# A first product with three tiles of the indexer's queries instead of two, in units of two k, and a smaller tile to warm TensorE

## The chip, the cores and the metric

The kernel runs on one core of one Trainium2 chip. A core has TensorE (PE in the profile, its weight loads PEld), VectorE (DVE), ScalarE (ACT), GpSimd (POOL) and SyncE (SP, here a queue that issues transfers). The metric is the device time of one execution in microseconds: 1672.79 us is the median of three runs before the change (1672.7 to 1672.99).

## The reference

One layer of a streaming encoder over 512 frames with 2048 channels, in float32. The normalised input goes through one wide projection, whose parts feed a sparse attention, a retention mixer and gates. The part that matters here is the indexer of the sparse attention: 16 heads of 64 channels (`iq`), one key of 64 channels (`ik`) and 16 weights (`iw`).

```python
h = rmsnorm(x, norm_gain)
proj = h @ w_in
(aq, ak, av, az, iq, ik, iw, rq, rk, rv, rz, ga, gb) = jnp.split(proj, SPLIT_POINTS, axis=-1)
...
iq = iq.reshape(B, L, IDX_HEADS, IDX_DIM) * (IDX_DIM ** -0.5)
ik = plain_layernorm(ik)
...
score = jnp.einsum('bqhd,bsd->bqsh', qi_c, ki)
index = jnp.einsum('bqsh,bqh->bqs', jax.nn.relu(score), w_c).astype(jnp.float32)
...
_, sel = lax.top_k(index, topk)
```

Behind it come the gather of the chosen keys, softmax, the retention, the output projections, a gated addition and a last RMSNorm.

## The kernel before

**Precision.** A float32 operand is split in two: `h`, the value rounded to the type that TensorE takes (`fp32r`), written by ACT (L153 for weights, L413 for the input), and `l`, the rest, written by DVE (L158, L414). A product is the sum of three matmuls: h with h, h with l, l with h (L214 to L216). `wh` and `wl` are the parts of a weight, `hh` and `hl` those of the input.

**Units.** Weights are loaded in units of some k (slices of 128 input channels, 16 in all). `block` registers the units of a matrix, `load_to` issues their transfers on SP's queue, and `split_to` emits the ACT instruction at once and the DVE one a step later. The raw tiles have 7 buffers (small units among the first four take another kind), `wh` and `wl` 3 each. `gemms` runs several products over the same input side by side: for each k it goes through its jobs, three matmuls each, and calls `step()` after each job. At the first k of a unit it splits units ahead: 2 from the current one in the first product, 3 in all others.

**Order.** The instructions of each engine run in the order in which this program emits them (`manual_schedule`), and each engine waits where an operand isn't ready. `todo` is a list from which each `step()` takes one entry (often empty); `later(n, f)` runs `f` n steps on; `bg` is a background list taken from when `todo` is empty.

**The head.** ACT's queue loads the gains; SP's queue loads the slices `xk` of the input and the units of `w_ik` in turn, in an order set by a list of k (L370). `w_ik` has 80 columns for the key and the weights and 256 for the first two tiles (of 128 columns, two heads) of the indexer's queries, in units of 1, 2, 2, 2, 3, 3 and 3 k. DVE sets `ones`, `mhalf` and `warm`; ten matmuls on `warm` (L408) keep TensorE busy until the first operands are there. `x_split` (L410) splits slice k of the input. Two slices and two units are split ahead of the first product; from there, the later slices stand in `todo`, a slice every three steps, with the squares for the RMSNorm between them (`rms_acc`).

The first product has three jobs: `ps_ikw` (80 columns, 512 frames) and two `ps_iq` (128 columns, the 384 frames for which a choice has to be made), so 9 matmuls and 3 steps a k. Then `kraw` is copied by ACT and each tile goes through `iq_split`: two ACT copies and two DVE subtractions. The six other tiles of the queries follow as products of their own, of 16 steps, in units of 8 k. Between them, from `todo`, come the sum of squares (`f_sum`), the RMSNorm's factor (`f_rnat`, `f_bcast`), the key's layernorm (`f_keys1` to `f_keys3`) and the scores of each tile (`index_tile`); by `later`, counted from the end of the first product, positions (`f_pos`), the bias table (`f_table1`, `f_table2`) and the rotary angles (`f_rope1`, `f_turns`, `f_rope2`). Then come the values (`ps_vn`), and the rest of the layer.

Of the kernel before, what the change touches and what calls it, by code (L numbers as in the profile page):

```python
# [11 lines left out]
BF = mybir.dt.bfloat16  # L12
# [5 lines left out]
L = 512  # L18
D = 2048
KT = D // 128  # L20
# [15 lines left out]
def block_kernel(tc, xT, pT, posb, posq, w_in, w_v, w_ik, w_a, w_b, w_o, w_ple, w_gate,  # L36
                 w_gt, w_pt, fgb, tab, gains, cst, dec, out, out_a, out_b):
    nc = tc.nc
    pe, dve, act, pool, sp = nc.tensor, nc.vector, nc.scalar, nc.gpsimd, nc.sync

    with contextlib.ExitStack() as ctx:
# [10 lines left out]
        def U(name, dt=F32):  # L52
            return up.tile([128, L], dt, name=name, tag="u")
# [26 lines left out]
        def block(src, chunks, cols=128):  # L80
            ids, k0 = [], 0
            for nk in chunks:
                ids.append(len(units))
                units.append((raw(src, k0, nk, cols), None, nk, cols))
                k0 += nk
            return ids
# [84 lines left out]
        todo = collections.deque()  # L171
# [27 lines left out]
        def gemms(jobs, ahead=None, order=None, each=None):  # L199

            pss = [P(j[4]) for j in jobs]
            seqs = [ksteps(j[0]) for j in jobs]
            late = order is not None
            order = order or range(len(seqs[0]))
            for s in order:
                for ps, seq, (_, w, parts, c, _) in zip(pss, seqs, jobs):
                    i, k = seq[s]
                    if k == 0:
                        split_to(i + (ahead or AHEAD) - (late and s > 0))
                        load_to(i + AHEAD + LOADS)  # L210
                    h, l = loaded[i]
                    a, b = parts[s][0][:, c], parts[s][1][:, c]
                    o = ps[:w.stop - w.start, c]
                    pe.matmul(o, h[:, k, w], a, start=(s == order[0]), stop=False)  # L214
                    pe.matmul(o, h[:, k, w], b, start=False, stop=False)  # L215
                    pe.matmul(o, l[:, k, w], a, start=False, stop=(s == order[-1]))  # L216
                    step()
                if each is not None:
                    each(s)
            return pss  # L220

        ALL = slice(0, L)
# [115 lines left out]
        K8 = (8, 8)  # L338
        col = lambda g, m: w_in[g + m]
        AQ, AK, AZ, IQ, RQ, RK, RZ, GA, GB = 0, 8, 16, 24, 32, 40, 48, 56, 72  # L340
        u_ik = block(w_ik, (1, 2, 2, 2, 3, 3, 3), 336)
        u_iq = [None, None] + [block(col(IQ, m), K8) for m in range(2, 8)]
        u_rv = [block(w_v[i], (2,) * 8, 512) for i in range(2)]
        u_av = block_wide_pair(w_v[2], w_v[3])
        u_r, u_g = [], []
        for h in range(NH):
            u_r.append(block_pair(col(RQ, h), col(RK, h)))
            for n in (2 * h, 2 * h + 1):
                g, m = ((GB, 2 * n), (GA, 2 * n - 16))[n >= 8]
# [17 lines left out]
        ng, fg, gn = g_sb[:, 0:16], g_sb[:, 16:32], g_sb[:, 32:40]  # L367
        xs = []
        for k in range(KT):
            if k in (1, 2, 3, 5, 7, 9, 12):  # L370
                load_to(state["raw"] + 1)
            if k < 10:
                t = U("xk")
                sp.dma_start(t, xT[:, k, :])
                xs.append(t)
            elif k % 2 == 0:
                t = B("xk2")
                sp.dma_start(t[:, 0:1024].rearrange("p (a c) -> p a c", a=2), xT[:, k:k + 2, :])
                xs += [t[:, 0:512], t[:, 512:1024]]
# [2 lines left out]
        pos_i = U("pos_i", I32)  # L382
        posq_i = cp.tile([128, 128], I32, name="posq_i")
        tb = cp.tile([128, 66], F32, name="tb")
        ones = cp.tile([128, 128], F32, name="ones")
        dve.memset(ones, 1.0)
        mhalf = cp.tile([128, 16], F32, name="mhalf")
# [5 lines left out]
        def rms_acc(src, k, c=ALL):  # L393
            sq = U("sq")
            act.activation(sq[:, c], src, AF.Square)
            i = k % 2
            if acc[i] is None:
                acc[i] = sq
            else:
                (pool, dve)[i].tensor_add(acc[i][:, c], acc[i][:, c], sq[:, c])  # L400

        warm = U("warm", BF)
        dve.memset(warm, 0.0)
        wact = cp.tile([128, 16], F32, name="wact")
        act.activation(wact, mhalf, AF.Copy)
        ps_w = P("ps_warm")
        for i in range(WARM):
            pe.matmul(ps_w, warm[:, 0:128], warm, start=(i == 0), stop=(i == WARM - 1))  # L408

        def x_split(k):  # L410
            h = U("hh", F32R)
# [37 lines left out]
        for k in range(2, KT):  # L449
            todo.append(lambda k=k: x_split(k))  # L450
            if k > 2:
                todo.extend([None, None if k % 2 else lambda k=k: rms_acc(xs[k // 2 - 2], k // 2 - 2)])
        for k in range(6, KT):
            todo.extend([lambda k=k: rms_acc(xs[k], k), None])

        ps_ikw, *ps_iq01 = gemms([(u_ik, slice(0, 80), hparts, ALL, "ps_ikw")]
                                 + [(u_ik, slice(a, a + 128), hparts, slice(128, L), "ps_iq") for a in (80, 208)], 2)

        def iq_split(ps):
            ta = U("ta", F32R)  # L460
# [7 lines left out]
        R = {}  # L468
        kraw = U("kraw")
        act.activation(kraw[:80, :], ps_ikw[:80, :], AF.Copy)  # L470
        ix = [iq_split(ps) for ps in ps_iq01]

        def f_sum():
            dve.tensor_add(acc[0], acc[0], acc[1])
# [119 lines left out]
            R["ct"], R["st"] = ct, st  # L594

        N3 = [None] * 3
        todo.extend(N3 * 3 + [f_sum] + N3 * 3 + [f_rnat] + N3 * 3 + [f_bcast, None, f_keys1] + N3 * 3 + [f_keys2] + N3 * 2 + [f_keys3] + N3 * 2)
        later(80, f_pos)
        later(88, f_table1)
        later(92, f_table2)  # L600
# [47 lines left out]
            load = [lambda: xn_load(k + 1)] if k < 7 else []  # L648
            return load + [lambda: xn_norm(k)] + [lambda i=i: h_step(k, i) for i in range(X_STEPS)]

        for m in range(2):
            index_tile(m, ix[m])
        for m in range(2, 8):
            ix = iq_split(gemm(u_iq[m], hparts, "ps_iq", slice(128, L)))
            index_tile(m, ix)

# [752 lines left out]
WARM = 10  # L1409
# [8 lines left out]
def _layout(x, p, positions, w_in, norm_gain, w_a_out, w_b_out, w_o, ret_gn_gain,  # L1418
            w_ple, w_ple_gate, rel_bias, final_gain):
    import numpy as np  # L1420
    f32 = np.float32

    def tiles(w, c=128):
        k, n = w.shape
        return np.ascontiguousarray(w.reshape(k // 128, 128, n // c, c).transpose(2, 1, 0, 3))

    def chans(v):
        return v.reshape(-1, 128).T

    w = np.asarray(w_in)[0]  # L1430
    o = {}
    o["xT"] = np.ascontiguousarray(np.asarray(x)[0].T.reshape(KT, 128, L).transpose(1, 0, 2))
    o["pT"] = np.ascontiguousarray(np.asarray(p)[0, 0].T.reshape(2, 128, L).transpose(1, 0, 2))
    pos = np.asarray(positions)[0]
    o["posb"] = np.ascontiguousarray(np.broadcast_to(pos[None, :], (128, L)))
    o["posq"] = np.ascontiguousarray(np.repeat(pos.reshape(128, 4).T, 32, axis=0))
    o["w_in"] = np.concatenate([tiles(w[:, a:b]) for a, b in
                                ((0, 2048), (3072, 5120), (5200, 7248), (8272, 13392))])
    o["w_v"] = np.concatenate([tiles(w[:, a:a + 1024], 512) for a in (7248, 2048)])
    o["w_ik"] = np.ascontiguousarray(  # L1440
        np.concatenate([w[:, 5120:5200], w[:, 4096:4352]], axis=1).reshape(KT, 128, 336).transpose(1, 0, 2))
    o["w_a"] = tiles(np.asarray(w_a_out)[0])
    o["w_b"] = tiles(np.asarray(w_b_out)[0])
    o["w_o"] = tiles(np.asarray(w_o)[0])
    o["w_ple"] = np.ascontiguousarray(
        np.asarray(w_ple)[0].reshape(2, 128, 16, 128).transpose(1, 2, 0, 3).reshape(128, 32, 128))
    o["w_gate"] = tiles(np.asarray(w_ple_gate)[0])
    o["w_gt"] = tiles(np.asarray(w_ple_gate)[0][:, 1536:], 512)
    o["w_pt"] = tiles(np.asarray(w_ple)[0][:, 1536:], 512)
    o["fgb"] = np.ascontiguousarray(np.broadcast_to(np.asarray(final_gain)[None, 1536:], (128, 512)))  # L1450
    tab = np.asarray(rel_bias)
    t = np.zeros((128, 66), f32)
    for q in range(4):
        for b in range(31):
            t[32 * q + b, 8 * q:8 * q + 8] = tab[ROW[b]]
            t[32 * q + b, 32 + 8 * q:40 + 8 * q] = tab[ROW[b - 1]]
        t[32 * q:32 * q + 32, 64] = [-1e9] + [i - 0.5 for i in THR[1:]] + [1e9]
        t[32 * q:32 * q + 32, 65] = [1.0] + [-1.0] * 31
    o["tab"] = t
    o["gains"] = np.ascontiguousarray(np.concatenate(  # L1460
        [chans(np.asarray(norm_gain)[0]), chans(np.asarray(final_gain)), chans(np.asarray(ret_gn_gain)[0])], axis=1))
    c = np.zeros((128, 130), f32)
    c[:, :128] = np.eye(128)
    c[:, 128] = np.tile((10000.0 ** (-np.arange(64) / 64.0)).astype(f32), 2)
    c[:, 129] = math.pi / 2
    o["cst"] = c
    s = np.arange(128)[:, None]
    q = np.arange(128)[None, :]
    dec = np.zeros((128, NH, 257))
    for h in range(NH):  # L1470
        g = math.log(1.0 - 2.0 ** (-5.0 - h))
        dec[:, h, :128] = np.where(q // 64 >= s // 64, np.exp(g * np.abs(q - s)), 0.0) * 128.0 ** -0.5
        dec[:, h, 128:256] = np.exp(g * (q + 1.0))
        dec[:, h, 256] = np.exp(g * (127.0 - s[:, 0])) * 128.0 ** -0.5
    o["dec"] = dec.astype(f32)
    return o
# [30 lines left out]
```

## Time and profile before

| | us |
|---|---|
| median of three runs | 1672.79 |
| profiled execution, its own time | 1672.5 |
| its span, first to last instruction | 1670.7 |
| PE busy | 1659.0 |
| DVE busy | 1255.5 |
| ACT busy | 934.8 |
| POOL busy | 251.7 |

Rows of the timeline give the start, the duration, engine, source line, operation, and output and inputs with shapes; in brackets stands how long the engine was idle before and what released it. The ends of matmuls are modelled and overlap the next one, so a rate is read from the starts. A row of the waits gives the total time, the number of waits and the longest one. A row of the windows gives, for a stretch of time, the busy time and count of PE, PEld, DVE, ACT and POOL, then the granted clock, the share of the DMA engines and GB/s. A row of the transfers gives their count, the size of one and the median time from issue to landing. Of the changes below, the profile's lines before L386 keep their numbers in the kernel after; those behind move by up to two.

### The profile page before, as it was taken

To read this page: it belongs to the slowest core of one execution; us is meant where nothing else is said; L and a number is where in the kernel's file an instruction comes from. 1 tells how busy PE (TensorE), PEld (TensorE's weight loads), DVE (VectorE), ACT (ScalarE), POOL (GpSimd) and SP (SyncE) were. 2 spreads that over 40 slices of the span, in tenths; PEclk is the share of its full clock that TensorE was granted. 3 is DMA by queue.
4 is the path that set the end of the run, shared out by engine and by line. 5 is a ranking of instruction groups with operands and counts; after the bars stand their busy time and mean duration, and the time that the engine had idled before them with its cause. 6 is when DMAs were issued, how large, how long until landed. Compare 5 with 4: busy or idle time off the path is not lost.

```text
span 1670.7 us, 24613 instructions
## 1 busy us (share of the span) xinstructions
PE 1659.0 (99%) x9160; PEld 1442.3 (86%) x9160; DVE 1255.5 (75%) x1912; ACT 934.8 (56%) x1424; POOL 251.7 (15%) x267
## 2 busy tenths in 40 slices
PE   9999999999999999999999999999999999999997
PEld 7988888888888888888888888888888888888896
DVE  7798789888888888777776676777678877864453
ACT  7465545555555555777766665566634544463342
POOL 2100112111111111111331112100000111012222
PEclk9999999999999999999999999999999999999998
DMA  7328989788788788788988888997466788732223
GB/s 290 127 89 256 321 233 275 189 209 218 193 205 216 192 204 217 192 228 243 239 236 221 220 223 226 255 363 276 150 227 189 194 215 221 203 107 101 88 64 101
DMA packets 122568, 343.26 MB, mean 205 GB/s; under 512 B 13712, under 2 KB 22800, under 8 KB 122448
## 3 DMA queue, kind: packets, MB, share of 16 engines
q1 hardware_dynamic: 85792, 229.98, 39.9%
q0 software_dynamic: 25712, 92.03, 29.3%
q10 hardware_dynamic: 10944, 19.69, 3.3%
q8 instruction: 72, 1.18, 0.3%
q14 instruction: 48, 0.39, 0.1%
HBM read 300.21 MB, written 41.42 MB: 204 GB/s over the span
## 4 chain that ended last, share of the span: by engine, by line
PE 95%; DVE 2%; ACT 2%; issue 1%; DMA 0%; POOL 0%; SPq 0%; POOLq 0%; ACTq 0%; DVEq 0%
PE ps_p L284 24%; PE ps_v L284 16%; PE ps_r L284 8%; PE ps_q L284 8%; PE ps_w L215 3%; PE ps_w L214 3%; PE ps_w L216 3%; PE ps_pg L216 3%; PE ps_pg L215 3%; PE ps_pg L214 3%; PE ps_vn L757 2%; PE ps_vn L758 2%; PE ps_vn L759 2%; PE ps_iq L214 1%; PE ps_iq L216 1%; PE ps_iq L215 1%
## 5 line engine op out<-in xcount | busy, mean ns | idle before, releaser
L158 DVE TENSOR_TENSOR wl<-wraw,wh 128x1024 fp32r<-128x1024 f32 (+2 forms) x459 | 563.0, 1239 | 176.2 <-ACT wh L153 174.5
L153 ACT ACTIVATE wh<-wraw 128x1024 fp32r<-128x1024 f32 (+2 forms) x459 | 474.4, 1043 | 234.4 <-DVE wraw L160 114.0
L119 POOL DMA_DIRECT2D wraw<-w_in x120 | 106.5, 958 | 572.2 <-DVE wl L158 321.1
L284 PE MATMUL ps_p<-hs,wh 128*128 128x512 f32 x640 | 161.4, 393 | 0.0
L247 ACT ACTIVATE e<-ps_p 128x512 f32<-128x512 f32 x144 | 86.0, 597 | 113.9 <-PE ps_p L284 112.5
L284 PEld LDWEIGHTS ps_p<-hs,wh 128*128 128x128 f32 x640 | 114.8, 189 | 21.0 <-issue 0.6
L284 PE MATMUL ps_p<-hs,wl 128*128 128x256 f32 x640 | 92.0, 284 | 0.0
L284 PEld LDWEIGHTS ps_p<-hs,wl 128*128 128x128 f32 x640 | 83.1, 192 | 0.3 <-issue 0.3
L284 PE MATMUL ps_q<-ha,wh 128*128 128x512 f32 x320 | 80.4, 393 | 0.0
L284 PE MATMUL ps_v<-ha,wh 128*128 128x512 f32 x320 | 80.1, 392 | 0.0
L284 PE MATMUL ps_r<-hs,wh 128*128 128x512 f32 x320 | 79.3, 390 | 0.4 <-ACT wh L153 0.4
L284 PE MATMUL ps_p<-ha,wh 128*128 128x512 f32 x320 | 79.6, 390 | 0.0
L284 PE MATMUL ps_v<-hs,wh 128*128 128x512 f32 x320 | 79.0, 389 | 0.0
L689 ACT ACTIVATE mk<-relf,thr 128x512 f16<-128x512 f32 (+3 forms) x128 | 68.2, 555 | 14.7 <-DVE go L977 10.2
L216 PE MATMUL ps_pg<-rh,wl 128*128 128x512 f32 x192 | 74.8, 390 | 0.0
L215 PE MATMUL ps_pg<-rl,wh 128*128 128x512 f32 x192 | 74.7, 389 | 0.0
L214 PE MATMUL ps_pg<-rh,wh 128*128 128x512 f32 x192 | 74.7, 389 | 0.0
L119 POOL DMA_DIRECT2D wraw<-w_o x24 | 21.1, 942 | 348.6 <-DVE wl L158 316.4
L977 DVE TENSOR_TENSOR go<-e_t 128x256 f32<-128x256 f32 x160 | 68.0, 425 | 5.7
L251 DVE TENSOR_TENSOR e_t<-ps_p,pv 128x512 f32<-128x512 f32 x48 | 33.1, 690 | 51.5 <-ACT e L247 51.5
L284 PEld LDWEIGHTS ps_r<-hs,wh 128*128 128x128 f32 x320 | 59.8, 188 | 13.8 <-ACT wh L153 1.4
L284 PEld LDWEIGHTS ps_p<-ha,wh 128*128 128x128 f32 x320 | 59.9, 188 | 13.0 <-issue 0.6
(412 smaller groups left out, 3739.2 us busy)
## 6 DMA issues: line engine op xcount, KB each, us to landing
wraw<-w_in SPq DMA_DIRECT2D x172, 512.0 KB, 5.2
wraw<-w_in POOLq DMA_DIRECT2D x120, 512.0 KB, 8.1
wraw<-w_v SPq DMA_DIRECT2D x32, 512.0 KB, 4.1
wraw<-w_o SPq DMA_DIRECT2D x32, 512.0 KB, 4.8
wraw<-w_o POOLq DMA_DIRECT2D x24, 512.0 KB, 6.3
wraw<-w_gate SPq DMA_DIRECT2D x24, 512.0 KB, 3.9
wraw<-w_b SPq DMA_DIRECT2D x16, 512.0 KB, 6.1
wraw<-w_a SPq DMA_DIRECT2D x16, 512.0 KB, 4.1
```

The costliest lines, as they stand in the source:

```text
L119: pool.dma_start(out=view(raw_tiles[r], nk, cols), in_=src[:, k0:k0 + nk, :], accum_op=OP.add)
L153: act.activation(h, raw, AF.Copy)
L158: dve.tensor_sub(l, raw, h.bitcast(F32))
L214: pe.matmul(o, h[:, k, w], a, start=(s == order[0]), stop=False)
L215: pe.matmul(o, h[:, k, w], b, start=False, stop=False)
L216: pe.matmul(o, l[:, k, w], a, start=False, stop=(s == order[-1]))
L247: act.activation(E[n], src, AF.Copy)
L284: pe.matmul(o[:, c], w[:, k], X[PRODUCTS[n]][k][:, c], start=(n < 4 and first and k == 0), stop=(ended[n] == 16), skip_group_check=True)
L689: act.activation(bias_e[b][:, ln * i:ln * i + ln], relf[:, :ln], AF.Sign, bias=thr[:, q:q + 1])
L757: pe.matmul(pss[t], a[:, tok(t)], h[:, k], start=(s == 0), stop=False)
L758: pe.matmul(pss[t], a[:, tok(t)], l[:, k], start=False, stop=False)
L977: dve.tensor_add(o[:, q], c0, c1)
```

## The change

A third tile of the indexer's queries (tile 2) is computed in the first product, which so has four jobs, 12 matmuls and 4 steps a k. The matrix `w_ik` is 464 columns wide instead of 336 and comes in units of 1, 1 and then seven times 2 k; the order of the loads follows. Tile 2 has no product of its own any more. The list of steps gets one empty step for each of the slices 3 to 7, and three empty steps fewer ahead of `f_sum`. `warm` is 128 columns instead of 512, is set first of DVE's tiles, and the warming matmuls read its 128 columns four times over.

```diff
-        u_ik = block(w_ik, (1, 2, 2, 2, 3, 3, 3), 336)
-        u_iq = [None, None] + [block(col(IQ, m), K8) for m in range(2, 8)]
+        u_ik = block(w_ik, (1, 1) + (2,) * 7, 464)
+        u_iq = [None] * 3 + [block(col(IQ, m), K8) for m in range(3, 8)]
...
-            if k in (1, 2, 3, 5, 7, 9, 12):
+            if k in (1, 2, 3, 5, 7, 9, 11, 13, 15):
                 load_to(state["raw"] + 1)
...
+        warm = U("warm", BF)[:, 0:128]
+        dve.memset(warm, 0.0)
         ones = cp.tile([128, 128], F32, name="ones")
         dve.memset(ones, 1.0)
...
-        warm = U("warm", BF)
-        dve.memset(warm, 0.0)
...
-            pe.matmul(ps_w, warm[:, 0:128], warm, start=(i == 0), stop=(i == WARM - 1))
+            pe.matmul(ps_w.rearrange("p (a c) -> p a c", a=4), warm, warm[:, None, :].to_broadcast([128, 4, 128]),
+                      start=(i == 0), stop=(i == WARM - 1))
...
-                todo.extend([None, None if k % 2 else lambda k=k: rms_acc(xs[k // 2 - 2], k // 2 - 2)])
+                todo.extend([None, None if k % 2 else lambda k=k: rms_acc(xs[k // 2 - 2], k // 2 - 2)] + [None] * (k < 8))
...
-        ps_ikw, *ps_iq01 = gemms([(u_ik, slice(0, 80), hparts, ALL, "ps_ikw")]
-                                 + [(u_ik, slice(a, a + 128), hparts, slice(128, L), "ps_iq") for a in (80, 208)], 2)
+        ps_ikw, *ps_iqs = gemms([(u_ik, slice(0, 80), hparts, ALL, "ps_ikw")]
+                                 + [(u_ik, slice(a, a + 128), hparts, slice(128, L), "ps_iq") for a in (80, 208, 336)], 2)
...
-        ix = [iq_split(ps) for ps in ps_iq01]
+        ix = [iq_split(ps) for ps in ps_iqs]
...
-        todo.extend(N3 * 3 + [f_sum] + N3 * 3 + [f_rnat] + N3 * 3 + [f_bcast, None, f_keys1] + N3 * 3 + [f_keys2] + N3 * 2 + [f_keys3] + N3 * 2)
+        todo.extend(N3 * 2 + [f_sum] + N3 * 3 + [f_rnat] + N3 * 3 + [f_bcast, None, f_keys1] + N3 * 3 + [f_keys2] + N3 * 2 + [f_keys3] + N3 * 2)
...
-        for m in range(2):
+        for m in range(3):
             index_tile(m, ix[m])
-        for m in range(2, 8):
+        for m in range(3, 8):
             ix = iq_split(gemm(u_iq[m], hparts, "ps_iq", slice(128, L)))
             index_tile(m, ix)
...
-        np.concatenate([w[:, 5120:5200], w[:, 4096:4352]], axis=1).reshape(KT, 128, 336).transpose(1, 0, 2))
+        np.concatenate([w[:, 5120:5200], w[:, 4096:4480]], axis=1).reshape(KT, 128, 464).transpose(1, 0, 2))
```

## The prediction

> **What bounds the kernel now.** I began with the page: its busy shares and its chain of waits.
>
> ```profile
> span 1670.7 us, 24613 instructions
> PE 1659.0 (99%) x9160; PEld 1442.3 (86%) x9160; DVE 1255.5 (75%) x1912; ACT 934.8 (56%) x1424; POOL 251.7 (15%) x267
> PE 95%; DVE 2%; ACT 2%; issue 1%; DMA 0%; POOL 0%; SPq 0%; POOLq 0%; ACTq 0%; DVEq 0%
> ```
>
> TensorE is the bound. A change that keeps its matmuls can only win back the 11.7 us in which PE is not busy (1670.7 less 1659.0), or open new waits. So the second view is PE's list of waits over the whole span, its three longest rows and the one of this stage:
>
> ```profile
> PE ps_b L1378 <- POOL rl L1374: 3.5, 1, 3.5
> PE ps_warm L408 <- DVE warm L403: 1.4, 1, 1.4
> PE ps_r L284 <- ACT wh L153: 0.4, 2, 0.2
> PE ps_ikw L216 <- DVE wl L158: 0.2, 1, 0.2
> ```
>
> The largest is in the tail, which the diff leaves alone. A busy PE hides waits for weights, so the third view is the timeline of the head, read by the starts of the matmuls.
>
> ```profile
> 0.84 0.17 DVE L386 MEMSET ones<- 128x128 f32 x1 [0.84 <-PEq L1498]
> 0.95 0.07 DVE L388 MEMSET mhalf<- 128x16 f32 x1
> 1.03 0.27 DVE L403 MEMSET warm<- 128x256 uint32 x1
> ...
> 1.36 4.45 PE L408 MATMUL ps_warm<-warm 128*128 128x512 bf16 x10 [1.36 <-DVE warm L403]
> ...
> 4.49 0.47 ACT L153 ACTIVATE wh<-wraw 128x336 fp32r<-128x336 f32 x1
> ...
> 5.17 0.25 PEld L214 LDWEIGHTS ps_ikw<-hh,wh 128*80 128x80 f32 x1 [0.28 <-ACT wh L153]
> ...
> 6.03 0.63 PE L215 MATMUL ps_ikw<-hl,wh 128*80 128x512 f32 x1
> 6.46 0.50 PE L216 MATMUL ps_ikw<-hh,wl 128*80 128x512 f32 x1
> ...
> 6.79 0.34 PE L214 MATMUL ps_iq<-hh,wh 128*128 128x384 f32 x1
> ...
> 7.20 0.77 ACT L153 ACTIVATE wh<-wraw 128x672 fp32r<-128x672 f32 x1 [1.15 <-DMA wraw<-w_ik]
> 8.00 0.86 DVE L158 TENSOR_TENSOR wl<-wraw,wh 128x672 fp32r<-128x672 f32 x1 [1.17 <-ACT wh L153]
> ...
> 8.91 0.46 PE L216 MATMUL ps_ikw<-hh,wl 128*80 128x512 f32 x1 [0.20 <-DVE wl L158]
> 9.21 0.34 PE L214 MATMUL ps_iq<-hh,wh 128*128 128x384 f32 x1
> 9.57 0.73 ACT L413 ACTIVATE hh<-xk,g_sb 128x512 fp32r<-128x512 f32 x1 [0.81 <-DMA xk<-xT]
> 10.21 0.75 ACT L153 ACTIVATE wh<-wraw 128x672 fp32r<-128x672 f32 x1
> 10.26 0.39 PE L214 MATMUL ps_ikw<-hh,wh 128*80 128x512 f32 x1
> ...
> 12.00 0.39 PE L214 MATMUL ps_ikw<-hh,wh 128*80 128x512 f32 x1
> ```
>
> Four readings. A 512-column matmul costs 0.43 us at first (6.03 to 6.46, and 4.45 over ten), so the warming ends about 1.36 + 4.27 = 5.63 and the real work starts near 5.60; TensorE runs at full speed from about 6.7. One k takes 1.74 us (10.26 to 12.00): three keys matmuls, 0.69 together, and two tiles at 0.52 each. Step k=0 should end at 6.79 + 1.05 = 7.84, and k=1 should reach its tiles at 7.84 + 0.69 = 8.53. They come at 9.21: **0.68 us lost**, to the second unit, which lands only at 7.20 and whose wl ends at 8.86. After that this stage loses nothing: k=2 lives on the same unit, and the third, split by ACT from 10.21 behind k=3's hh, is wanted only at 12.00.
>
> **The change part by part.** *Tile moved.* 48 matmuls of 384 columns move from a product of their own into the first one; none is added. In both places three take 0.52 us, and the 16 slices of 128 columns to split replace two units of 1024. In matmul time: 0.
>
> *Warming.* A memset of 64 words lies between those of 16 (0.07) and 128 (0.17): 0.11. It is now first, from 0.84, so it ends at 0.95, and with the 0.06 that the row shows up to the matmul the warming starts at 1.01 and ends at 5.28, 0.35 earlier. But the first unit is now 464 columns wide. Its split, between 0.47 (336) and 0.77 (672), takes 0.58, so from 4.49 it ends at 5.07; before, 4.96 was followed by matmuls only at 5.60 because of the warming. Adding the 0.2 until PE's weight load begins and the 0.25 of the load, work starts at 5.52. **Gain 0.08 us** (bounds 0 and 0.35). That the ten matmuls read one block four times has no row; I take 0.43 each, since the number of columns is the same. Doubled, it would cost 4.3 us.
>
> *Units of (1, 1, 2, ...).* With three tiles a k takes 1.74 + 0.52 = 2.26 us. k=0 runs from 5.52: 1.19 as before until its tiles (5.60 to 6.79), then 1.57, so to 8.28. The second unit is smaller (cumulated 976 KB to its end, against 1016), so its wh is ready by 7.8 and its wl by 8.5, before the third matmul of k=1 at 8.74: **the old 0.68 goes**. k=1 ends at 10.54. Now k=2 needs the *third* unit, and ACT's order is still hh of k=2, hh of k=3, then this wh.
>
> ```profile
> 8.00:10.00 2.00, 1.78 (x9) 1.26 (x9) 1.55 (x2) 1.15 (x2) 0.00 (x0) 1.00 1.03 393
> ...
> wraw<-w_ik SPq DMA_DIRECT2D x3, 336.0 KB, 5.8
> ...
> wraw<-w_ik SPq DMA_DIRECT2D x1, 168.0 KB, 3.0
> ...
> 15.09 1.03 ACT L153 ACTIVATE wh<-wraw 128x1008 fp32r<-128x1008 f32 x1
> 16.15 1.21 DVE L158 TENSOR_TENSOR wl<-wraw,wh 128x1008 fp32r<-128x1008 f32 x1 [0.18 <-ACT wh L153]
> ```
>
> The x of k=3 landed at 9.57 after 4 x 256 + 168 + 336 + 336 = 1864 KB; now 1952 KB go ahead, and 88 KB at 393 GB/s are 0.23 us: 9.80. The wh follows 0.64 later (9.57 to 10.21), at 10.44, and for 928 columns (between 0.75 and 1.03) takes 0.97: 11.41. PE, ready at 10.54, starts k=2 at about 11.46: **0.92 us lost**. The wl then takes 1.12 (between 0.86 and 1.21), to 12.57; by the row of before the tiles follow 0.35 after a wl's end (8.86 to 9.21), at 12.92 instead of 11.46 + 0.69 = 12.15: **0.77 us lost**. Behind this ACT and DVE have 4.5 us for each unit and need about 3.3, so nothing more. Balance of the head: -0.08 - 0.68 + 0.92 + 0.77 = **+0.93 us** (bounds -0.76, if the third unit came in time, and +1.7, if both matmul waits were half as long again).
>
> *The turn into the next product.* Only one unit of it is split ahead; the second waits behind what is done with the first product's results.
>
> ```profile
> 33.84 0.59 ACT L470 ACTIVATE kraw<-ps_ikw 80x512 f32<-80x512 f32 x1 [5.33 <-PE ps_ikw L216]
> ...
> 34.68 0.35 PE L214 MATMUL ps_iq<-hh,wh 128*128 128x384 f32 x1
> ...
> 35.38 0.55 DVE L464 TENSOR_TENSOR ta<-ps_iq,ta 64x384 fp32r<-64x384 f32 x1 [2.51 <-ACT tz L463]
> ...
> 37.67 2.36 DVE L158 TENSOR_TENSOR wl<-wraw,wh 128x1024 fp32r<-128x1024 f32 x2
> ...
> 39.21 0.33 PE L216 MATMUL ps_iq<-hh,wl 128*128 128x384 f32 x1
> ```
>
> Count from the end T of the first product (34.68). DVE's first subtraction starts at T + 0.70, four take 2.29, the first of two wl ends at T + 4.17, and the matmul that reads it starts at T + 4.53: 0.36 spare, about 0.2 of it the weight load. With a third tile the keys' result is ready 0.52 earlier before T, so the first subtraction starts at T + 0.18; six take 3.43, and the wl ends at T + 4.79. Queued behind these subtractions are this wl and the next; PE waits for the first: 0.26 + 0.2 = **0.45 us lost** (bounds 0 and 1.1, two subtractions' time). The next unit has a further 4 us.
>
> *Shifts behind it.* Position, table and rotary steps are counted from the end of the first product and come 16 steps later; the index tasks behind them by 2.
>
> ```profile
> 57.44 1.05 PE L432 MATMUL ps_bc<-cs,r_nat 128*128 128x128 f32 x8
> ...
> 84.17 0.42 DVE L538 CAST relf<-rel_i 128x512 f32<-128x512 int32 x1
> ...
> 85.47 0.20 DVE L547 MAX8 d<-da 128x8 f32<-128x32 f32 x1
> ...
> 88.96 0.38 PE L554 MATMUL ps_d<-cs,d 128*128 128x128 f32 x2
> ...
> 119.79 0.41 DVE L593 TENSOR_SCALAR st<-st 64x512 f32<-64x512 f32 x1
> ...
> 100.00:110.00 10.00, 10.00 (x49) 8.43 (x48) 9.50 (x15) 4.48 (x9) 0.00 (x0) 1.00 0.35 106
> ```
>
> The matmul on the table has 3.3 us of cover and keeps its eight steps. DVE is 95% busy in the values' stage, into which these steps move, but PE does not wait there: nothing, as long as the split units ahead cover it. SP's constants now stand behind two more weight loads, some 2 us, against a first use at 57.44. Of the 0.4 us of waits at ps_r, a shifted order could remove all or add as much: 0 taken.
>
> **Sum.** +0.93 + 0.45 = +1.4 us. The profiled execution took 1672.5 us (1.8 around its span of 1670.7), 0.3 below the median of 1672.79. Against that median: **1674.2 us, 0.08% more**, within the 0.2% (3.3 us) that a measurement here tells from no change.
>
> **The rivals.** *The third unit arrives in time.* For it: DMA moves faster than the bytes ask once running, and the early units of weights come in longer rows. Against: x of k=3 waited for its DMA, and ACT works in order. If the waits at k=2 vanish, -0.76 + 0.45 = -0.3: 1672.5 us.
>
> *The clock falls back.* Waits of 0.92 and 0.77 us within 2.4 us, just after full speed was reached, could return TensorE to half speed. The first rise took from 1.36 to about 6.7, 5.3 us; as long again at half speed costs 2.65, so 1674.2 + 2.65 = 1676.9, slower than before. [...] Against it: before, 0.68 us idle at 8 us left the spacing at 0.17. The Trainium skill (TensorE: Matmul & The Clock Gate, "Why this matters for your kernels") asks for idle gaps of over about 3 us before the rate halves; by that rule neither gap is enough and the sum stays 1674.2.
>
> *The values' stage falls behind.* The steps that move there, from the row at 84.17 to the one at 119.79, are 26 instructions of DVE with 9.4 us together. If DVE's idle 5% doesn't absorb them in time and a wl comes late by a third of it, 3 us: 1677. Against it: units there are split three ahead, and the steps leave a stage where DVE was as full.
>
> **How the numbers follow.** Forecast 0.62 (own range 1673.3 to 1675.3, from the bounds at k=2 and the turn), third unit in time 0.18, clock 0.09, values' stage 0.08, anything else 0.03. Faster by over 0.2% needs more than the head ever lost: 0.02. Slower by over 0.2% (above 1676.1) takes the two slow rivals and the forecast's upper edge, 0.09 + 0.08 + 0.03 = 0.20; within is 0.78. The range 1672.2 to 1676.6 holds the forecast and the first rival, and leaves most of the slow ones out.
>
> **What would show it.** Right: warming from about 1.0 us; no gap at k=1; k=2's first matmul near 11.5, behind ACT's wh, its tiles near 12.9; the first product ending near 43.9 us; a short PE wait on wl some 4.5 us after. Wrong: k=2 back to back, spacing of 0.43 us after 12 us, or PE waits past 90 us that were not there.

## The result and the profile after

| | before | after |
|---|---|---|
| median of 21 runs each | 1672.60 us | 1675.36 us |
| lowest to highest | 1671.77 to 1673.34 | 1674.48 to 1676.10 |
| profiled execution: its own time, span | 1672.5, 1670.7 | 1675.02, 1673.3 |

The ratio is 1.0016, 95% interval 1.0010 to 1.0022: the change costs 2.8 us. The forecast had +1.4 us. The page of the kernel after says what still bounds it:

```profile
span 1673.3 us, 24614 instructions
PE 1659.8 (99%) x9160; PEld 1441.9 (86%) x9160; DVE 1252.7 (75%) x1912; ACT 933.6 (56%) x1424; POOL 250.2 (15%) x267
```

The count of matmuls is the same and PE is busy 0.8 us more; the other 1.8 of the 2.6 us of span are new idle time. PE's list of waits over the whole span of the kernel after tells where (total us, count, longest):

```profile
PE ps_b L1379 <- POOL rl L1375: 3.5, 1, 3.5
PE ps_r L284 <- ACT wh L153: 1.4, 3, 0.7
PE ps_warm L408 <- DVE warm L386: 1.0, 1, 1.0
PE ps_ikw L216 <- DVE wl L158: 0.5, 1, 0.5
PE ps_ikw L214 <- ACT wh L153: 0.3, 1, 0.3
PE ps_iq L216 <- DVE wl L158: 0.2, 1, 0.2
```

The tail's 3.5 is unchanged and the warming's wait is shorter. The rows of `ps_ikw` and `ps_iq` are the head and the turn, which the prediction had. The row it took at nothing is the second: `ps_r`, one of the paired products (L284) far behind the edit, waits 1.4 us in place of 0.4. The weight loads show the same at more places; their rows of the same view, before and then after:

```profile
PEld ps_r L284 <- ACT wh L153: 1.4, 3, 0.6
```

```profile
PEld ps_r L284 <- ACT wh L153: 3.4, 5, 1.2
```

**The head.** The timeline of the kernel after:

```profile
1.00 4.45 PE L408 MATMUL ps_warm<-warm 128*128 128x512 bf16 x10 [1.00 <-DVE warm L386]
...
6.09 0.45 PE L216 MATMUL ps_ikw<-hh,wl 128*80 128x512 f32 x1
...
6.39 0.34 PE L214 MATMUL ps_iq<-hh,wh 128*128 128x384 f32 x1
...
8.65 0.34 PE L214 MATMUL ps_iq<-hh,wh 128*128 128x384 f32 x1
...
9.02 0.72 ACT L414 ACTIVATE hh<-xk,g_sb 128x512 fp32r<-128x512 f32 x1 [1.16 <-DMA xk<-xT]
...
9.65 0.96 ACT L153 ACTIVATE wh<-wraw 128x928 fp32r<-128x928 f32 x1
...
10.06 0.34 PE L216 MATMUL ps_iq<-hh,wl 128*128 128x384 f32 x1
...
10.64 1.13 DVE L158 TENSOR_TENSOR wl<-wraw,wh 128x928 fp32r<-128x928 f32 x1
...
10.66 0.46 PE L214 MATMUL ps_ikw<-hh,wh 128*80 128x512 f32 x1 [0.27 <-ACT wh L153]
...
11.82 0.46 PE L216 MATMUL ps_ikw<-hh,wl 128*80 128x512 f32 x1 [0.48 <-DVE wl L158]
...
12.12 0.34 PE L214 MATMUL ps_iq<-hh,wh 128*128 128x384 f32 x1
```

The tiles of k=0 come at 6.39, where before had 6.79; those of k=1 at 8.65, with no gap; k=2 starts at 10.66 instead of 10.06 + 0.17 = 10.23, behind ACT's wh, and its tiles at 12.12 instead of 10.66 + 0.69 = 11.35, behind DVE's wl. So k=2 loses 0.43 + 0.77 = 1.20 us.

**The turn.** The timeline of the kernel before, at the first matmul behind its third tile (48 matmuls behind 34.68), and then that of the kernel after, at the same place of the work:

```profile
43.03 0.33 PE L214 MATMUL ps_iq<-hh,wh 128*128 128x384 f32 x1
...
1659.52 0.39 PE L1313 MATMUL ps_tw<-wh,pl 128*128 128x512 f32 x1
```

```profile
43.15 0.33 PE L214 MATMUL ps_iq<-hh,wh 128*128 128x384 f32 x1
...
46.74 2.36 DVE L158 TENSOR_TENSOR wl<-wraw,wh 128x1024 fp32r<-128x1024 f32 x2
...
47.48 0.34 PE L215 MATMUL ps_iq<-hl,wh 128*128 128x384 f32 x1
...
48.02 0.44 PE L216 MATMUL ps_iq<-hh,wl 128*128 128x384 f32 x1 [0.20 <-DVE wl L158]
...
1661.64 0.39 PE L1314 MATMUL ps_tw<-wh,pl 128*128 128x512 f32 x1
```

Read by the starts of the same matmul, the head costs 43.15 - 43.03 = 0.12 us, and the turn 48.02 - 47.66 = 0.36 (47.66 is one spacing of 0.18 behind 47.48). At the last matmul before the tail the lag is 1661.64 - 1659.52 = 2.12 us. So **1.64 us are lost between 50 and 1660 us**, where no matmul was touched. The last 0.4 of the 2.6 lie in the tail behind that matmul: 11.2 us before and 11.6 after. In the profiled executions of the runs below the same stretch takes 10.7 to 11.6, without a pattern, so I read nothing into it. These are single executions: at the first of these matmuls, two with the same head differ by up to 0.28 us, as the part on the prediction shows.

**The middle.** The timelines around one wait, first before, then after. DVE's rows are a top-k round (MAX8, MATCH_REPLACE8), `go` is the result of a paired product, `rb` a copy of it by ACT, and the wh is the one that `ps_r` needs:

```profile
347.68 0.42 DVE L672 MAX8 m<-isc 128x8 f32<-128x256 f32 x1
...
348.21 0.41 DVE L673 MATCH_REPLACE8 isc<-m,isc 128x256 f32<-128x256 f32 x1
...
354.74 0.42 DVE L977 TENSOR_TENSOR go<-e_t 128x256 f32<-128x256 f32 x1
...
355.20 0.63 ACT L788 ACTIVATE rb<-go 64x512 f32<-64x512 f32 x1 [2.63 <-DVE go L977]
...
356.50 1.06 ACT L153 ACTIVATE wh<-wraw 128x1024 fp32r<-128x1024 f32 x1
...
357.71 2.00 PE L284 MATMUL ps_r<-hs,wh 128*128 128x512 f32 x8
```

```profile
347.88 0.69 DVE L673 MAX8 m<-isc 128x8 f32<-128x512 f32 x1
...
348.68 0.68 DVE L674 MATCH_REPLACE8 isc<-m,isc 128x512 f32<-128x512 f32 x1
...
355.47 0.42 DVE L978 TENSOR_TENSOR go<-e_t 128x256 f32<-128x256 f32 x1
...
355.93 0.63 ACT L789 ACTIVATE rb<-go 64x512 f32<-64x512 f32 x1 [2.63 <-DVE go L978]
...
357.23 1.06 ACT L153 ACTIVATE wh<-wraw 128x1024 fp32r<-128x1024 f32 x1
...
358.34 1.90 PE L284 MATMUL ps_r<-hs,wh 128*128 128x512 f32 x7 [0.27 <-ACT wh L153]
```

In the same place stands a round of 256 columns before and one of 512 after. It is 0.54 us longer, and DVE makes none of it up on the way to `go`: its one pause there, of 0.21 us before and 0.20 after, is for ACT's copies of an earlier `go`, which wait for DVE in their turn. ACT's two copies wait for `go`, and the wh stands behind them in ACT's order: 0.73 us later (356.50 to 357.23), of which 0.20 is the lag that was there already. The wh had almost no spare, and PE restarts at 358.34, with a lag of 0.63 in place of 0.20.

The lag behind the kernel before changes at five places, and these make up the 1.64 to within 0.1: it is 0.46 us at 290 us, 0.20 behind 295 (a wait of the kernel before that is gone), 0.76 behind 358, 0.48 behind 607 (gone again), 1.51 behind 671 and 2.18 behind 737. Not all of them are a round that met another length. At 671, the largest, the last round of 512 columns and its scaling to the mask (L676) stand where the kernel before, whose rounds are over, has mask steps of ACT (`mk`). At 737 it is a mask step of ACT that stands right ahead of the wh:

```profile
661.84 0.43 DVE L676 TENSOR_SCALAR mneg<-isc 128x512 bf16<-128x512 f32 x1
...
671.26 2.11 PE L284 MATMUL ps_r<-hs,wh 128*128 128x512 f32 x8 [0.74 <-ACT wh L153]
...
734.92 0.72 ACT L690 ACTIVATE mk<-relf,thr 128x512 f16<-128x512 f32 x1
```

Why other entries stand there: `todo` received five empty entries (one for each k from 3 to 7) and lost three in the list behind the product. Index tasks come two steps later, as the prediction said, and the background list, which is only served when `todo` is empty and in this stage at every second step, loses one turn. From there on each of its entries stands one place later. Its rounds go through tiles of 256, 384 and 512 columns in turn, so every place meets another length, and they end one place later.

### The profile page after: what moved, and what is told of

Same layout as the page of the kernel before. It is cut to its first block, busy times and chain, and to the rows that moved or that the text cites. A ratio compares the mean times of both kernels' runs of the same rounds, so it can differ in the third digit from the quotient of the medians.

```text
span 1673.3 us, 24614 instructions
## 1 busy us (share of the span) xinstructions
PE 1659.8 (99%) x9160; PEld 1441.9 (86%) x9160; DVE 1252.7 (75%) x1912; ACT 933.6 (56%) x1424; POOL 250.2 (15%) x267
## 4 chain that ended last, share of the span: by engine, by line
PE 92%; DVE 3%; ACT 2%; issue 1%; DMA 1%; SPq 0%; POOL 0%; ACTq 0%; POOLq 0%; DVEq 0%
PE ps_p L284 23%; PE ps_v L284 15%; PE ps_r L284 8%; PE ps_q L284 8%; PE ps_w L215 3%; PE ps_w L214 3%; PE ps_w L216 3%; PE ps_pg L216 3%; PE ps_pg L214 3%; PE ps_pg L215 3%; PE ps_vn L758 2%; PE ps_vn L760 2%; PE ps_vn L759 2%; PE ps_iq L216 1%; PE ps_iq L214 1%; PE ps_iq L215 1%
## 5 line engine op out<-in xcount | busy, mean ns | idle before, releaser
L158 DVE TENSOR_TENSOR wl<-wraw,wh 128x1024 fp32r<-128x1024 f32 (+3 forms) x459 | 558.6, 1230 | 174.9 <-ACT wh L153 172.6
L153 ACT ACTIVATE wh<-wraw 128x1024 fp32r<-128x1024 f32 (+3 forms) x459 | 473.8, 1042 | 224.6 <-DVE wraw L160 114.2
L284 PE MATMUL ps_p<-hs,wh 128*128 128x512 f32 x640 | 161.4, 394 | 0.0
L284 PEld LDWEIGHTS ps_p<-hs,wh 128*128 128x128 f32 x640 | 114.8, 189 | 20.9 <-issue 0.4
L284 PE MATMUL ps_p<-hs,wl 128*128 128x256 f32 x640 | 92.0, 284 | 0.0
L284 PEld LDWEIGHTS ps_p<-hs,wl 128*128 128x128 f32 x640 | 83.1, 192 | 0.3 <-issue 0.3
L284 PE MATMUL ps_r<-hs,wh 128*128 128x512 f32 x320 | 79.7, 391 | 1.4 <-ACT wh L153 1.4
L284 PE MATMUL ps_q<-ha,wh 128*128 128x512 f32 x320 | 80.4, 392 | 0.0
L284 PE MATMUL ps_v<-ha,wh 128*128 128x512 f32 x320 | 80.3, 393 | 0.0
L284 PE MATMUL ps_p<-ha,wh 128*128 128x512 f32 x320 | 79.3, 389 | 0.0
L284 PE MATMUL ps_v<-hs,wh 128*128 128x512 f32 x320 | 79.0, 389 | 0.0
L284 PEld LDWEIGHTS ps_r<-hs,wh 128*128 128x128 f32 x320 | 59.7, 188 | 15.6 <-ACT wh L153 3.4
L284 PEld LDWEIGHTS ps_p<-ha,wh 128*128 128x128 f32 x320 | 60.0, 188 | 12.8 <-issue 0.4
```

What stands on the lines that cost most here:

```text
L153: act.activation(h, raw, AF.Copy)
L158: dve.tensor_sub(l, raw, h.bitcast(F32))
L284: pe.matmul(o[:, c], w[:, k], X[PRODUCTS[n]][k][:, c], start=(n < 4 and first and k == 0), stop=(ended[n] == 16), skip_group_check=True)
```

## The experiments

Theory 1: this shift of the background by one entry costs some 1.7 us, as waits of `ps_r` for wh. Theory 2: the loss in the middle comes from the moved table and rotary steps, from the weights' buffers or from the transfers. "ps_tw" in the tables is the start in the profiled execution of the last matmul before the tail (1659.52 before, 1661.64 after), "ratio" is against the kernel before on the same chip.

### The list alone, and the two waits alone

e1, on the changed kernel:

```diff
-        bg.extend([lambda: None] * 4)
+        bg.extend([lambda: None] * 3)
```

> The changed kernel with one empty entry fewer (three instead of four) at the head of the background list, so that the top-k rounds and the mask steps stand again where the kernel before has them among the paired products' steps. Theory 1 (some 1.7 us of the loss come from that list standing one entry later, and are lost as waits of the gate product ps_r for ACT's wh): about 1.6 us less than the changed kernel, 1673.7; the waits at 357.7 and 670.1 us go and those of the kernel before, at about 294.7 and 606.8, come back; the lag behind the kernel before stays near 0.5 us from 125 us to the end of the products. Theory 2 (the loss in the middle comes from the table and rotary steps, from the slots of the weights or from the transfers): no change, 1675.4, and the lag still grows at 358, 670 and 736 us.

e2, on the kernel before:

```diff
-        bg.extend([lambda: None] * 4)
+        bg.extend([lambda: None] * 5)
```

> The kernel before with one empty entry more (five instead of four) at the head of the background list; nothing else of the change. Theory 1: the list alone costs some 1.7 us, so about 1674.2 against 1672.6, with waits of ps_r near 357, 670 and 736 us as the changed kernel has them. Theory 2: the order of the background is worth nothing, 1672.6.

e3, on the changed kernel:

```diff
-            todo.append(lambda k=k: x_split(k))
+            todo.append(lambda k=k: (x_split(k), k == 2 and split_to(3)))
```

> The changed kernel with the third unit of the first product split by ACT ahead of its hh of k=3 instead of behind it. If the waits at k=2 (0.43 and about 0.8 us after 10 us) come from ACT's order, as the prediction had it: wh starts near 9.1 us or as soon as the unit has landed, k=2 follows k=1 without a gap, and the first product ends about 1.2 us earlier, near 42.0; the time falls by as much, to 1674.2, if nothing behind it shifts against the background. Rival (the third unit itself lands late, and ACT's order is no matter): wh starts near 9.6 us as in the changed kernel, hh of k=3 comes later, and the time stays within 0.2 us of 1675.4.

e4, on the changed kernel:

```diff
-                        split_to(i + (ahead or AHEAD) - (late and s > 0))
+                        split_to(i + (ahead or AHEAD) - (late and s > 0) + (ahead is not None and i == seq[-1][0]))
```

> The changed kernel with a second unit of the next product split ahead at the last step of the first, so that its wl stands in front of the six subtractions on DVE. If the wait of 0.36 us at 47.7 us comes from the wl behind six subtractions, as the prediction had it: it goes, and the time falls by some 0.4 us, to 1675.0. Rival (the wl in front delays the subtractions, and with them the keys' steps or the release of the three results' buffers): the wait is replaced by one of another row near 45 to 60 us, and the time stays or rises.

| run | median us (11 runs; before 1672.67) | ratio, 95% interval | ps_tw |
|---|---|---|---|
| e1 | 1673.43 | 1.0005 [0.9996, 1.0014] | 1660.03 |
| e2 | 1674.35 | 1.0011 [1.0002, 1.0020] | 1661.35 |
| e3 | 1674.03 | 1.0010 [1.0001, 1.0019] | 1660.63 |
| e4 | 1674.71 | 1.0014 [1.0005, 1.0023] | 1661.16 |

e1 and e2 settle the middle. One empty entry fewer takes 1.93 us from the changed kernel's median of 1675.36 (1.61 by `ps_tw`); one more adds 1.68 to the kernel before (1.83 by `ps_tw`). PE's waits, e1 first, then e2:

```profile
PE ps_r L284 <- ACT wh L153: 0.4, 2, 0.2
```

```profile
PE ps_r L284 <- ACT wh L153: 1.4, 3, 0.7
```

e1 has the row of the kernel before, e2 that of the changed kernel. The starts of `ps_r` behind these waits say the same: at 295.25 and 607.41 us before, 295.74 and 607.95 in e1; at 358.34, 671.26 and 736.64 after, 358.02, 670.95 and 736.35 in e2. Theory 2 expected no effect of either, and falls. What e1 keeps, 1660.03 - 1659.52 = 0.51 us, is the head and the turn (0.12 + 0.36).

e3, with the third unit in front, has these rows in its timeline:

```profile
8.67 0.98 ACT L153 ACTIVATE wh<-wraw 128x928 fp32r<-128x928 f32 x1 [0.49 <-DMA wraw<-w_ik]
...
10.23 0.39 PE L214 MATMUL ps_ikw<-hh,wh 128*80 128x512 f32 x1
...
10.86 0.46 PE L216 MATMUL ps_ikw<-hh,wl 128*80 128x512 f32 x1
...
11.16 0.33 PE L214 MATMUL ps_iq<-hh,wh 128*128 128x384 f32 x1
```

The unit had landed by 8.67, a microsecond before ACT came to it in the changed kernel. k=2 starts on time at 10.23, and its tiles at 11.16 instead of 12.12: 0.96 us back, short of the expected 1.2 because the wl still makes the third matmul wait. `ps_tw` is 1.01 earlier, so it is kept to the end; the median fell by 1.33. The rival, that the unit itself lands late, is out.

In e4 the matmul that waited in the changed kernel follows one spacing behind that at 47.40, on the timeline of PE:

```profile
47.58 0.33 PE L216 MATMUL ps_iq<-hh,wl 128*128 128x384 f32 x1
```

There is no wait, and none took its place: 0.48 us by `ps_tw`, of which 0.08 was there in the head before the turn; 0.65 by the median.

### The warming alone, all edits, and other places of the list

e5, on the kernel before, only this of the change:

```diff
+        warm = U("warm", BF)[:, 0:128]
+        dve.memset(warm, 0.0)
...
-        warm = U("warm", BF)
-        dve.memset(warm, 0.0)
...
-            pe.matmul(ps_w, warm[:, 0:128], warm, start=(i == 0), stop=(i == WARM - 1))
+            pe.matmul(ps_w.rearrange("p (a c) -> p a c", a=4), warm, warm[:, None, :].to_broadcast([128, 4, 128]),
+                      start=(i == 0), stop=(i == WARM - 1))
```

> The kernel before with the change to the warming alone: its 128 columns are set first, and the ten matmuls read them four times over. The prediction had this part at a gain of 0.08 us with the changed units, because the first unit then ends the warming's cover. Here the first unit is the old one (wh ended at 4.96 in the kernel before, the work began behind the warming at 5.60): the work should begin about 5.3, TensorE should reach its full speed about 0.35 us earlier (6.3 instead of 6.66), and, if the second unit then sets k=1 as before (its wl ended at 8.86), nothing of it is left behind k=1: 1672.6, within 0.2 us. Rival (the earlier clock is a gain of its own that stays): 0.3 us less, 1672.3.

e6 is the changed kernel with the edits of e1, e3 and e4 together; e7 has two empty entries in place of e6's three (first pair of lines), e8 six (second pair):

```diff
-        bg.extend([lambda: None] * 3)
+        bg.extend([lambda: None] * 2)
...
-        bg.extend([lambda: None] * 3)
+        bg.extend([lambda: None] * 6)
```

> The changed kernel with the three edits together: the third unit ahead of hh of k=3, a second unit of the next product split ahead, and three empty entries at the head of the background list. Theory 1, by the sums of the single edits (1.34 + 0.65 + 1.93 by the medians, 0.98 + 0.5 + 1.6 by the starts of the same matmuls): 1675.4 less 3.1 to 3.9, so 1671.5 to 1672.3, below the kernel before (1672.67) by 0.4 to 1.2 us. Theory 2 (the edits overlap, one wait stands behind the other): 1673 or above.

> The same three edits, with two empty entries instead of three. If theory 1 is right in its mechanism (a top-k round of DVE ahead of the steps that release ACT's copies delays the wh for ps_r, and the three sizes of round follow one another in a cycle of three entries), every place in the paired products meets another size of round than with three or with four entries: the waits at 294.7 and 606.8 us and those at 357.7 and 670.1 us change, and the time moves by 0.5 to 2 us against three entries, to either side. Theory 2 (only the place of four entries is a bad one, for another reason): the same time as with three, within 0.2 us.

> The same three edits, with six empty entries. By the cycle of three, each place among the products meets the same size of round as with three entries as long as the rounds last (to about 700 us): the same waits of ps_r near 294 and 606 us and none at 357; behind them only the mask steps stand three entries later. So the same lag as with three entries up to 660 us, and a difference of up to 1 us afterwards. Rival (the number of the entry itself decides, not the cycle): another set of waits before 660 us.

| run | median us (10 to 11 runs; before 1672.46) | ratio, 95% interval | ps_tw | starts of `ps_r` behind a wait |
|---|---|---|---|---|
| e5 | 1672.42 | 1.0000 [0.9991, 1.0009] | 1660.04 | as before |
| e6 | 1671.85 | 0.9995 [0.9986, 1.0004] | 1658.83 | 294.56, 606.72 |
| e7 | 1670.97 | 0.9991 [0.9982, 1.0000] | 1657.80 | none |
| e8 | 1672.62 | 1.0001 [0.9992, 1.0010] | 1659.68 | 294.25, 606.42, 733.42 |

e5 is worth nothing in the median, as expected. Its `ps_tw` is 0.52 us later than that of the kernel before, but this is the head of one execution: the second unit let its wh start at 7.83, not 7.20. The timeline shows why an earlier start of the work isn't kept:

```profile
0.99 4.26 PE L408 MATMUL ps_warm<-warm 128*128 128x512 bf16 x10 [0.99 <-DVE warm L386]
...
5.09 0.46 PE L214 MATMUL ps_ikw<-hh,wh 128*80 128x512 f32 x1
...
7.83 0.76 ACT L153 ACTIVATE wh<-wraw 128x672 fp32r<-128x672 f32 x1 [1.19 <-DMA wraw<-w_ik]
...
8.65 0.46 PE L214 MATMUL ps_ikw<-hh,wh 128*80 128x512 f32 x1 [1.22 <-ACT wh L153]
```

TensorE is at full speed with the first product's first matmul (0.46 long, where 6.03 before was 0.63), but k=1 waits for the second unit, which set the head before, too.

In e6 the gains add, nearly: 1675.36 - 1671.85 = 3.5 us by the medians, where the three sum to 3.9, and 2.8 by `ps_tw`, where they sum to 3.1. e7 and e8 bear the cycle out. With six entries the waits up to 660 us are those of three; behind the rounds, where mask steps take over, the two part: a wait at 733.42 comes in, and the time is 0.77 us higher (by the starts of the same matmuls e8 falls back by 1.2 us behind 660 us: 0.4 at 669, where the weight load of `ps_r` waits 0.50 us, and 0.7 at this wait). With two entries the places meet other lengths, no wait of `ps_r` on PE is left, and the time falls by 0.88.

### The length of a round, and the kernel before in the best place

e9, on the changed kernel, in each top-k round (it leaves out the rounds of the two larger tiles, so its choice of keys is not that of the other kernels):

```diff
-            a = R["isc"][:, IOFF[t]:IOFF[t] + 128 * (t + 1)]
+            a = R["isc"][:, IOFF[1]:IOFF[1] + 256]
             m8 = S("m8", 8)
             dve.max(m8, a)
             dve.match_replace(out=a, in_to_replace=m8, in_values=a, imm_value=-3.39e38)
+            a = R["isc"][:, IOFF[t]:IOFF[t] + 128 * (t + 1)]
```

> The changed kernel, order and entries untouched, with every top-k round run over the 256 columns of the smallest tile, so that the rounds of the two larger tiles are left out (48 rounds of some 0.9 us of DVE stay). Theory 1 (the length of the round that stands ahead of DVE's go decides): the wait of ps_r at 357.7 us, behind a round of 512 columns, goes (0.4 to 0.6 us); that at 670.1, behind the last round and its scaling to the mask, falls from 0.90 to 0.1 to 0.5 us; that at 736, behind ACT's mask step, stays: 0.8 to 1.1 us less in all, 1674.4. Rival (the number of the entry decides and not its length): waits and time as in the changed kernel, 1675.4.

e10 is the kernel before with three empty entries instead of four, e11 is e7 again.

> The kernel before with one empty entry fewer (three), which puts its background where the kernel with all three edits has it with two entries. Theory 1: the two waits of ps_r at 294.7 and 606.8 us go and no other comes, 0.96 us less by the starts of the same matmuls: 1671.5. Rival (the gain with two entries hung on the other edits): 1672.5.

> The three edits with two empty entries once more, beside the kernel before with its background in the same place: 1671.0 again. If the unit of three tiles brings something of its own once its waits are gone (0.69 us by the starts of the same matmuls with three entries), it is below the kernel before with three entries (1671.5) by 0.5 to 0.9 us; if not, both are alike within 0.2 us.

| run | median us (11 runs; before 1672.50) | ratio, 95% interval | ps_tw |
|---|---|---|---|
| e9 | 1673.45 | 1.0006 [0.9997, 1.0014] | 1659.82 |
| e10 | 1672.42 | 1.0000 [0.9991, 1.0009] | 1658.83 |
| e11 | 1670.80 | 0.9991 [0.9982, 1.0000] | 1657.73 |

In e9 not one entry is moved, and 1.9 us go (1.82 by `ps_tw`, of which 0.2 lie in the head). Its waits of PE and of the weight loads:

```profile
PE ps_r L284 <- ACT wh L153: 0.4, 1, 0.4
```

```profile
PEld ps_r L284 <- ACT wh L153: 1.5, 3, 0.8
```

The one wait left on PE is that at 734.8 us, behind ACT's mask step, which was expected to stay. I had expected 0.8 to 1.1 us. By the starts of the same matmuls 0.54 us come back at 358 and 0.63 of 1.03 at 671, as expected (a weight load still waits 0.52 there). What I hadn't counted are two small waits of the weight loads, at 295 and 608 (0.24 and 0.21), and the 0.2 of the head. So it is the length of the work ahead on DVE that decides at four of the five places. e9 by itself can't tell a short round ahead of `go` from a DVE that is less busy everywhere; e1, e2 and e7, which move the waits with the same work, show that the place matters.

e10 misses its expectation. Both waits of `ps_r` are gone from its trace and `ps_tw` is 0.69 us earlier, but the median is only 0.08 below. Its profiled execution, at 1671.62, is the shortest of its eleven; what the others lost no trace shows. That stays open. e11 repeats e7: 1.6 us below e10, where 0.5 to 0.9 were expected (1.10 by `ps_tw`, and all of that is there at the first matmul behind the third tile, which starts at 41.80 in e11 and 42.90 in e10). So the changed first product, with its third unit in front, does win something: this matmul starts at 41.80 to 42.42 us in the four traces that have it so beside the second unit split ahead (e6, e7, e8, e11), and at 42.90 to 43.18 in the three with the old head.

## Why the prediction was right, and by how much not

**Right in direction, and in size partly by luck.** The measured 2.8 us lie just above the forecast's own range (1675.3, or +2.5 at most). They lie inside 1672.2 to 1676.6 because that range is wide and because two errors partly cancel: head and turn cost 0.9 us less than forecast, and a term put at nothing cost 1.6. With that term taken out (e1) the ratio is 1.0005, with an interval from 0.9996 to 1.0014, so by the medians even the direction hangs on it. No rival named this cause, and one of the signs given for being wrong did come: PE waits past 90 us that were not there.

The places in the head and the turn were right, and TensorE's order stays the bound. No gap at k=1, k=2 behind ACT's wh and then DVE's wl, and the short wait on wl some 4.5 us behind the first product are in the trace as described.

**The head: +0.93 forecast, +0.12 measured.** The wait of the tiles on the wl came out at 0.77, as worked out. (The upper bound, with both waits half as long again, comes to +1.8 and not +1.7.) Two terms were mis-sized. The start at k=2: 0.92 forecast, 0.43 measured, because x of k=3 had landed by 9.02 and not 9.80 (k=1 also ended earlier, at 10.23 and not 10.54, which takes back 0.31); I had put the 88 KB more behind the arrival of before, but the transfers ran faster than before. The windows of 6 to 7 us, before and then after (last number GB/s):

```profile
6.00:7.00 1.00, 1.00 (x5) 0.75 (x4) 0.75 (x1) 0.05 (x1) 0.00 (x0) 1.00 0.99 364
```

```profile
6.00:7.00 1.00, 1.00 (x6) 0.95 (x6) 0.75 (x1) 0.73 (x2) 0.00 (x0) 1.00 1.05 417
```

This is no chance of one execution: with 88 KB more ahead of it, x of k=3 lands at 8.77 to 9.53 us in the nine traces with the new units, and at 9.32 to 10.02 in the four with the old ones. Why they run faster, no run shows.

The warming: a gain of 0.08 forecast; the tiles of k=0 came 0.40 earlier (6.39 against 6.79), as TensorE reached its full speed near 6.1 instead of 6.7. That is chance and not the edit: in e2 and e10, whose head is that of the kernel before, the tiles came at 6.21 and 6.20. It gains nothing either way, since the second unit sets k=1: its tiles come at 9.21, 9.40 and 9.12 in before, e2 and e10. In the changed kernel they come at 8.65, with a third tile of 0.52 done by then. That the ten matmuls read one block four times costs nothing: they took 4.45 us in both.

With the old 0.68 gone: -0.40 - 0.68 + 0.43 + 0.77 = +0.12. The first matmul behind the third tile starts at 43.03, 43.18 and 42.90 with the old head (before, e2, e10) and at 43.15, 43.17 and 42.93 with the new one (changed kernel, e1, e9). So these traces don't tell the new head as a whole from the old one.

**The turn: +0.45 forecast, +0.36 measured**, by the mechanism described; e4 removes it.

**The shifts behind: 0 forecast, +1.64 measured.** This is the step of the prediction that failed: "a shifted order could remove all or add as much: 0 taken". The bound of 0.4 us came from the waits that before happened to have, and a schedule whose spare is near zero in many places has no such bound: the loss after depends on which entry meets which place. It removed the two waits of the kernel before and brought three larger ones. That the index tasks come two steps later was on record; that this is one turn of the background for the rest of the products was not followed. The moved table and rotary steps themselves cost nothing: with the list put back, e1 stays within a few hundredths of a lag of 0.5 us from 120 us to the end of the products.

**The rivals.** The third unit was not in time (e3 shows what that would have been worth, 0.96 us). The clock did not fall back: behind 12.12 the spacing is 0.17 again, after gaps of 0.43 and 0.77 us. This agrees with the rule of the Trainium skill that the prediction weighed (TensorE: Matmul & The Clock Gate, "Why this matters for your kernels"). The values' stage did not fall behind. So the loss is twice the forecast although head and turn cost 0.48 us in place of 1.38: the step taken as zero outweighs them. Together the three make 2.1 of the 2.8 us. Some 0.4 of the rest lie in the tail, where no run shows a cause.

## What to carry to other kernels

Where a hand-made order has almost no spare, an edit at one end shifts everything that is counted in steps behind it: count the entries added and removed, and if they don't cancel, expect a change of the order of the whole schedule's slack, with either sign. Before crediting or blaming an edit, put the order behind it back (one empty entry here): this change costs 2.8 us as written, some 0.8 with the list in its old place (its interval includes no loss at all), and with its two own waits removed and the list one place further it runs 1.5 to 1.7 us below the kernel before (ratio 0.9991, with an interval from 0.9982 to 1.0000). Two instructions in the wrong order on an engine can be worth more than the bytes that they wait for: in e3 the third unit's data was there a microsecond before the changed kernel took it up.

## What the runs showed of the hardware

The time from the start of the warming to full speed is not fixed. The ten warming matmuls started at 0.99 to 1.00 us in these three executions of the same warming, e1, e5 and the changed kernel. The rows of the last two are above; that of e1 is

```profile
0.99 3.78 PE L408 MATMUL ps_warm<-warm 128*128 128x512 bf16 x10 [0.99 <-DVE warm L386]
```

Ten at 0.43 would take 4.3 and more. In e1 full speed came inside the warming, after some 3.0 us: its ninth matmul starts at 4.18, only 0.22 behind the eighth. In the changed kernel it came after 5.1 (1.00 to 6.1), and in the kernel before after 5.3 (1.36 to 6.7). In e2 and e10, with the same warming as the kernel before, it came after some 3.5, as the tenth matmul starts 0.31 and 0.26 behind the ninth. The shortest of the thirteen traces is e7 with 2.9, the longest e6 with 5.9. The granted clock in the rows of the windows doesn't show this: it is 1.00 in the kernel before in every microsecond from 1 to 10, so the speed has to be read from the spacing. The early one won nothing, since the weights of the first unit set the start of the work. The arrival of the same early transfer varies too: the second unit of `w_ik` let its wh start at 7.20 in the kernel before, at 7.39 and 7.11 in e2 and e10, and at 7.83 in e5, which all issue the same transfers. A difference of half a microsecond in the head between two single executions says little.
